# A hand-planned decoder trunk on one core: whole PSUM banks as dependences, top-k steps moved between two attentions, and a planned margin on results that TensorE takes

## The chip, the cores and the metric

The kernel runs on one core of a Trainium2 chip. The metric is the device time of one execution in microseconds (us). Engines: TensorE (PE; PEld is its weight load), VectorE (DVE), ScalarE (ACT), GpSimd (POOL) and SyncE (SP), which here issues DMAs. TensorE writes its results to PSUM, which has eight banks of 512 floats per partition; VectorE and ScalarE read them there.

## The reference

A decoder trunk of two layers over 512 positions with a residual stream of 1024 channels, in float32. Each layer does, on the normalised stream:

```python
z = rmsnorm(x, norm_g[i]) @ w_in[i]          # one projection, split into all inputs below
o_a = diff_attention(...)     # A: 4 heads, each softmax map 0 - lam * softmax map 1, RMSNorm per head
o_b = dsa_attention(...)      # B: an indexer scores the keys, top 128 of them per query, 8 heads
o_c = nsa_attention(...)      # C: compressed blocks + selected blocks + window, 8 heads, sigmoid gates
up = einsum('bsnw,nwd->bsnd', stack([o_a*silu(a_g), o_b*silu(b_g), o_c*silu(c_g)], 2), w_up[i])
x = x + sum(sigmoid(merge) * up, axis=2) @ w_out[i]
x = x + (p[i] @ w_ple[i]) * sigmoid(rmsnorm(x, ple_norm_g[i]) @ w_ple_gate[i])
```

The top 128 keys of B are found by 16 rounds that take the eight largest scores of each query and strike them out.

## The kernel before

The stream lies transposed, channels on partitions, in eight tiles of 128 x 512. Every float32 operand of a large matmul is split into a high and a low part (`whi`, `wlo` for weights, `HI`, `LO` for the stream, `PTh`, `PTl` for probabilities), and a product is three matmuls. The high part of a weight is a copy by ScalarE or GpSimd, the low part a subtraction by GpSimd or VectorE.

The order of work is written by a planner, `Plan`. The kernel's text records operations in a sequence (`add`), with a cost for each and the operations it must come after; that is found from boxes (`box`: partitions from and to, columns from and to) of the cells that each operation reads or writes in a tile (`meet`). Writers and readers whose boxes meet are ordered. All TensorE operations on one tile are ordered anyway (`filler`). Then `put_down` (line 387) makes the time table: at each step it takes the operation that can start earliest on any engine; for engines other than TensorE a rank (its place in the sequence) is added with a small weight, TensorE takes of the ready ones that with the lowest rank. `o.ready` is the planned time at which an operation may start, set by the ends of those it depends on; a tile's slot in a ring of buffers is released apart from that. An operation listed for two engines (`VG`: GpSimd or VectorE, `AG`: ScalarE or GpSimd) goes to the one that would end it first. The table's order of each engine is what the chip runs; semaphores for the true dependences are added when the operations are put down.

The sequence of a layer: projections for the indexer and the token values; `index_scores`; `attend_a` for four heads (A); `attend_c` for four tiles of queries with two groups and two maps each (C); `attend_b` for four pairs of heads (B); then output projections. Each attention is woven (`weave`) with projections that do not depend on it (`proj`, `merge`, `rise`), in `mm` banks (3), while the attention's scores, transposes and sums take `at` banks (5).

Places that the prediction speaks of. `weigh_a`, inside `attend_a` (from line 1085), transposes a head's probabilities and sums the values into one bank `po`, four blocks of 128 columns by 1, 2, 3 and 4 matmuls (two records each in the trace); ScalarE reads each block into `o`, squares it, GpSimd makes the inverse root (`rsqrt`), ScalarE scales `o`, and later `turn` transposes it:

```python
T.matmul(po[:, i * P : (i + 1) * P], at[:, j * P : (j + 1) * P],
         AV[j][:, h * P : (h + 1) * P], start=j == 0, stop=j == i)
...
A.activation(on[:, i * P : (i + 1) * P], po[:, i * P : (i + 1) * P], AF.Copy,
             scale=rr[:, 0, i : i + 1])
```

`topk` (line 1059) is a generator of 51 steps a layer: 48 of a maximum and a replacement on VectorE (16 rounds over three blocks of queries), and three that turn the marks into masks for B. `background(n)` (line 1072) takes n of them, with the rank set back by 400; `attend_a` calls it with `A_TOPK[i]` for each query block i of a map, `softmax` with `C_TOPK[i]` in C. What is left is taken before `attend_b`. `c_query` writes an unrotated query `t` by VectorE and multiplies it with the compressed keys (`at<-KCb,t`).

Of the kernel before, what the change touches and what calls it, by code (L numbers as in the profile page):

```python
# [25 lines left out]
ROUNDS = 16  # L26
NQB = 6
PV_LAG = 3
A_TOPK = (0, 0, 1, 1)
C_TOPK = (0, 0, 1, 1)  # L30
NRAW = 4
NWS = 4
NKB = 10
URGE = 0.002
WARM = 9
THETA = 500000.0

# [89 lines left out]
class View:  # L127
# [23 lines left out]

    def box(self):

        a, b = int(self.cells[(0,) * self.cells.ndim]), int(self.cells[(-1,) * self.cells.ndim])
        w = self.tile.width
        return a // w, b // w, a % w, b % w
# [7 lines left out]
    def put_down(self):  # L164
        x = self.tile.put_down()
        for kind, a, b in self.steps:
            if kind == "getitem":
                x = x[a]
            elif kind == "rearrange":
                x = x.rearrange(a, **b)  # L170
            elif kind == "bitcast":
                x = x.bitcast(a)
            else:
                x = x.to_broadcast(a)
        return x
# [43 lines left out]
class Plan:  # L219
# [52 lines left out]
    def add(self, names, call, args, kw):  # L272
# [15 lines left out]
        for x in op.ins:  # L288
            box = x.box()
            for b, w in x.tile.writes:  # L290
                if self.meet(b, box):
                    op.after.add(w)
        for x in op.outs:
            box, t = x.box(), x.tile
            for line in (t.writes, t.reads):
                for b, w in line:
                    if self.meet(b, box):
                        op.after.add(w)
# [88 lines left out]
    def put_down(self):  # L387
        names = ("tensor", "vector", "scalar", "gpsimd", "sync")
        free = dict.fromkeys(names, 0.0)
        port = wire = 0.0  # L390
        held = {(e, o.seq): self.shares(e, o) for o in self.ops for e in o.engines}

        def begin(e, op):
            at = max(free[e], op.ready)
            return max(at, port - 0.14) if held[e, op.seq] else at

        can = {e: [] for e in names}
        slots = {r: [(0.0, k) for k in range(self.size[r])] for r in self.rings}
        line = {r: list(t) for r, t in self.rings.items()}

        def enter(op):
            if op.left == 0:
                for e in op.engines:
                    can[e].append(op)

        def give(ring):
            while line[ring] and slots[ring]:
                t = line[ring].pop(0)
                at, t.slot = min(slots[ring])
                slots[ring].remove((at, t.slot))  # L410
                for op in t.users:
                    op.ready = max(op.ready, at)
                    op.left -= 1
                    enter(op)

        def finish(e, op):

            at = begin(e, op) + self.cost(e, op)[0]
            return at + sum(o.us for o in can[e] if o.rank < op.rank and len(o.engines) == 1 and o.ready <= at)

        for r in line:
            give(r)
        done = 0
        while done < len(self.ops):
            best = None
            for e in names:
                pick = None
                for op in can[e]:
                    at = begin(e, op)
                    key = at + (0.0 if e == "tensor" else URGE) * op.rank  # L430
                    if pick is not None and (pick[2], pick[1].rank) < (key, op.rank):
                        continue
                    if len(op.engines) > 1 and e != min(op.engines, key=lambda x: finish(x, op)):
                        continue
                    pick = (at, op, key)
                if pick and (best is None or pick[0] < best[0]):
                    best = (pick[0], e, pick[1])
            if best is None:
                raise RuntimeError("the plan is stuck")
            at, e, op = best  # L440
            us, lag = (op.us, op.lag) if e == op.engines[0] else self.cost(e, op)
            op.engine, op.start = e, at
            free[e] = at + us
            if held[e, op.seq]:
                port = at + us
            for x in op.engines:
                can[x].remove(op)
            done += 1
            end = at + us + lag
            if op.call == "dma_start":  # L450
                tile = (op.outs + op.ins)[0]
                end = wire = max(end, wire) + 0.1 + tile.shape[0] * tile.columns() * 4 / 370000.0
            for o in op.next:
                o.ready = max(o.ready, at + us if o.engines == (e,) and op.call != "dma_start" else end)
                o.left -= 1
                enter(o)
            for t in op.tiles.values():
                t.uses -= 1
                t.end = max(t.end, end)
                if t.uses == 0 and t.space != "dram":  # L460
                    slots[t.ring].append((t.end, t.slot))
                    give(t.ring)
        E = mybir.EngineType
        with self.tc.manual_schedule(engines={E.PE, E.DVE, E.Activation, E.Pool, E.SP}):
            for op in sorted(self.ops, key=lambda o: (o.start, o.seq)):
                real = [a.put_down() if isinstance(a, View) else a for a in op.args]
                kw = {k: a.put_down() if isinstance(a, View) else a for k, a in op.kw.items()}
                call = op.call
                if call == "copy" and op.engine == "gpsimd":
                    call, real = "tensor_scalar", real + [1.0, 0.0, ALU.mult, ALU.add]  # L470
                getattr(getattr(self.nc, op.engine), call)(*real, **kw)  # L471
# [3 lines left out]
def trunk_kernel(ctx, tc, xT, xN, pT, pos, freq, W, WK, small, con, out):  # L475
# [38 lines left out]
    def at_ps():  # L514
        return ps("at", 5)
# [18 lines left out]
    spare = at_ps()  # L534
    for _ in range(WARM):
        T.matmul(spare[:, :P], ones, ones, start=True, stop=True)
# [125 lines left out]
    for l in range(L):  # L662
# [178 lines left out]
        def causal(i):  # L841
            return mask[:, 384 - i * P : 512]

        def softmax_parts(pt, i, sc, m, st):

            n = P * (i + 1)
            blk = pt[:, POFF[i] : POFF[i] + n]
            mn = sb("mx", (P, 1), bufs=8)
            V.tensor_tensor_reduce(blk, sc[:, :n], m, 1.0, -NEG, ALU.add, ALU.min, mn)
            A.activation(blk, blk, AF.Exp, bias=mn, scale=-1.0, accum_out=st[:, i : i + 1])  # L850
# [221 lines left out]
        def background(n):  # L1072

            plan.shift = 400
            for _ in range(n):
                next(chain, None)
            plan.shift = 0
# [7 lines left out]
        def attend_a(h):  # L1085
            pts, sts = [], []
            for c in range(2):
                pt = sb("P", (P, 1280), bufs=3)
                st = sb("st", (P, NQ), bufs=4)
                for i in range(NQ):  # L1090
                    sc = sc_ps()
                    qk(sc, have["AQ", h][c], have["AK", h, c], i)
                    softmax_parts(pt, i, sc, causal(i), st)
                    background(A_TOPK[i])
                    yield QK_US[i]
# [64 lines left out]
        def softmax(q, k, masks, factor):  # L1160
# [3 lines left out]
            for i in range(NQ):  # L1164
# [3 lines left out]
                if masks is masks_c:  # L1168
                    background(C_TOPK[i])
                yield QK_US[i]  # L1170
# [359 lines left out]
```

## Time and profile before

| | before |
|---|---|
| time, median of 3 runs | 1411.82 us (1410.4 to 1412.04) |
| the profiled execution | 1409.82 us |
| its span, first to last instruction | 1408.0 us |
| TensorE busy, instructions | 1378.9 us (98%), 6882 matmul records |
| VectorE busy | 1046.4 us (74%) |
| ScalarE busy | 790.3 us (56%) |
| GpSimd busy | 567.3 us (40%) |

All rows come from the one profiled execution. Nearly every operation is recorded by one helper line, so groups are told apart by tile names ("out<-in"). A matmul's recorded length is longer than its distance to the next, since matmuls are pipelined; a stall shows as a larger distance between starts, and in part as idle time.

### The profile page before, as it was taken

Reading aid. Unit: us, or ns where it says so; the run is one execution under the profiler, and the core shown is the slowest. Engines: PE = TensorE matmul, PEld = TensorE weight load, DVE = VectorE, ACT = ScalarE, POOL = GpSimd, SP = SyncE. Lnnn points to the kernel's source line nnn. Section 1 sums busy time; section 2 is a strip of 40 time slices with the busy share of each in tenths; the row PEclk is TensorE's granted clock in tenths of the full one; section 3 lists DMA queues with packets and bytes.
Section 4 is the critical chain, followed back from the end, with each engine's and each line's share of the span. In section 5 each row is a group of like instructions: output and inputs, shape, how many; then the busy total and the mean of one; then the engine's idle time right before and its main releaser. Section 6 shows DMA issues by size and latency. Waiting matters only on the chain.

```text
span 1408.0 us, 20777 instructions
## 1 busy us (share of the span) xinstructions
PE 1378.9 (98%) x6882; PEld 1153.3 (82%) x6882; DVE 1046.4 (74%) x2348; ACT 790.3 (56%) x1831; POOL 567.3 (40%) x613
## 2 busy tenths in 40 slices
PE   9999999999999999999999999999999999999997
PEld 7888877888888888888887888778888888888886
DVE  7688888888887566555785888897888855666566
ACT  6455655866764356334444656567677734643443
POOL 3464466545343152122251744774445322313040
PEclk9999999999999999999999999999999999999998
DMA  6223221111222221342422231312112222124221
GB/s 246 98 83 101 72 89 62 61 61 53 75 68 83 85 88 61 106 149 98 147 83 97 83 98 52 106 55 67 60 61 68 76 83 89 62 75 157 97 91 68
DMA packets 67932, 123.65 MB, mean 88 GB/s; under 512 B 7920, under 2 KB 10224, under 8 KB 67824
## 3 DMA queue, kind: packets, MB, share of 16 engines
q1 hardware_dynamic: 62640, 113.14, 24.5%
q10 hardware_dynamic: 5184, 9.18, 1.9%
q8 instruction: 54, 0.88, 0.2%
q14 instruction: 54, 0.44, 0.1%
HBM read 117.57 MB, written 4.72 MB: 87 GB/s over the span
## 4 chain that ended last, share of the span: by engine, by line
PE 89%; DVE 5%; ACT 1%; issue 1%; POOL 0%; DMA 0%; DVEq 0%; POOLq 0%; ACTq 0%; SPq 0%
PE mm L471 70%; PE at L471 19%; DVE t L471 1%; DVE nt L471 0%; DVE P L471 0%; POOL nt L471 0%; DVE cm L471 0%; DMA raw<-W 0%; DVE K L471 0%; DVE rstd L471 0%; ACT o L471 0%; DVE g L471 0%; DVE wlo L471 0%; DVE x L471 0%; DVE hr L471 0%
## 5 line engine op out<-in xcount | busy, mean ns | idle before, releaser
L471 PE MATMUL mm<-HI,whi 128*128 128x512 f32 x1240 | 496.9, 401 | 2.1 <-POOL whi L471 1.1
L471 PE MATMUL mm<-HI,wlo 128*128 128x512 f32 x1240 | 488.7, 394 | 1.6 <-DVE wlo L471 1.0
L471 PE MATMUL mm<-LO,whi 128*128 128x512 f32 x1240 | 488.0, 394 | 1.3 <-DVE LO L471 1.3
L471 POOL TENSOR_SCALAR whi<-raw 128x512 fp32r<-128x512 f32 (+1 forms) x191 | 130.5, 684 | 535.2 <-PE mm L471 357.2
L471 POOL TENSOR_TENSOR wlo<-raw,whi 128x512 fp32r<-128x512 f32 (+1 forms) x191 | 256.9, 1348 | 188.0 <-ACT whi L471 151.6
L471 PEld LDWEIGHTS mm<-HI,wlo 128*128 128x128 f32 x1240 | 233.9, 189 | 51.0 <-DVE wlo L471 1.4
L471 PEld LDWEIGHTS mm<-HI,whi 128*128 128x128 f32 x1240 | 234.3, 189 | 41.8 <-POOL whi L471 1.6
L471 ACT CAST whi<-raw 128x512 fp32r<-128x512 f32 (+1 forms) x205 | 125.2, 614 | 254.8 <-PE mm L471 185.5
L471 PEld LDWEIGHTS mm<-LO,whi 128*128 128x128 f32 x1240 | 234.4, 189 | 40.0 <-DVE LO L471 2.3
L471 DVE TENSOR_TENSOR wlo<-raw,whi 128x512 fp32r<-128x512 f32 (+1 forms) x205 | 149.7, 735 | 79.6 <-ACT whi L471 43.9
L471 ACT ACTIVATE P<-P,mx 128x512 f32<-128x512 f32 (+3 forms) x256 | 142.4, 557 | 65.7 <-DVE mx L471 64.6
L471 PE MATMUL at<-K,Q 128*128 128x256 f32 (+3 forms) x608 | 138.9, 325 | 0.0
L471 PEld LDWEIGHTS at<-K,Q 128*128 128x128 f32 x608 | 103.1, 189 | 16.1 <-issue 0.5
L471 DVE TENSOR_TENSOR t<-mm,R 128x512 f32<-128x512 f32 (+1 forms) x101 | 69.0, 683 | 61.1 <-PE mm L471 57.8
L471 DVE CUSTOM_DVE_ANT_0 P<-at,consts 128x128 f32<-128x128 f32 x208 | 93.8, 470 | 21.6 <-PE at L471 20.5
L471 DVE TENSOR_TENSOR PTl<-at,PTh 128x512 fp32r<-128x512 f32 x192 | 87.0, 484 | 28.2 <-ACT PTh L471 21.6
L471 POOL TENSOR_TENSOR Q<-t,Q 64x512 fp32r<-64x512 f32 x64 | 87.5, 1367 | 34.9 <-ACT Q L471 29.3
L471 PE MATMUL at<-consts,P 128*128 128x128 f32 x560 | 96.1, 272 | 0.8 <-ACT PTh L471 0.7
L471 ACT ACTIVATE P<-P,rc 128x128 f32<-128x128 f32 x192 | 92.0, 552 | 7.9 <-DVE rc L471 6.9
L471 ACT CAST PTh<-at 128x512 fp32r<-128x512 f32 x192 | 74.4, 420 | 38.4 <-PE at L471 31.1
L471 PEld LDWEIGHTS at<-consts,P 128*128 128x128 f32 x560 | 71.5, 140 | 22.1 <-ACT PTh L471 1.3
L471 PE MATMUL mm<-BRh,whi 128*128 128x512 f32 x192 | 77.0, 405 | 0.5 <-DVE t L471 0.5
(222 smaller groups left out, 2126.5 us busy)
## 6 DMA issues: line engine op xcount, KB each, us to landing
raw<-W SPq DMA_DIRECT2D x396, 256.0 KB, 2.6
raw<-WK SPq DMA_DIRECT2D x16, 176.0 KB, 2.3
X<-xT ACTq DMA_DIRECT2D x10, 256.0 KB, 4.1
res<-X ACTq DMA_DIRECT2D x8, 256.0 KB, 2.0
X<-res ACTq DMA_DIRECT2D x8, 256.0 KB, 3.4
out<-K SPq DMA_DIRECT2D x8, 256.0 KB, 2.5
X<-xT SPq DMA_DIRECT2D x6, 256.0 KB, 4.8
P<-xN SPq DMA_DIRECT2D x3, 512.0 KB, 6.0
```

The costliest lines, as they stand in the source:

```text
L471: getattr(getattr(self.nc, op.engine), call)(*real, **kw)
```

## The change

Three edits. A PSUM tile's box is now the whole tile, so a read of some of its columns depends on earlier writes of others. The selection takes no step in A, and three steps a map instead of two in C. In the time table an operation of TensorE that depends on one of VectorE, ScalarE or GpSimd is ready 0.6 us after the planned end of that one.

```diff
-A_TOPK = (0, 0, 1, 1)
-C_TOPK = (0, 0, 1, 1)
+A_TOPK = (0, 0, 0, 0)
+C_TOPK = (0, 1, 1, 1)
...
+SLACK = 0.6
...
     def box(self):
 
+        if self.tile.space == "psum":
+            return 0, self.tile.shape[0] - 1, 0, self.tile.width - 1
         a, b = int(self.cells[(0,) * self.cells.ndim]), int(self.cells[(-1,) * self.cells.ndim])
...
             for o in op.next:
-                o.ready = max(o.ready, at + us if o.engines == (e,) and op.call != "dma_start" else end)
+                late = SLACK if o.engines[0] == "tensor" and e in ("vector", "scalar", "gpsimd") and op.call != "dma_start" else 0.0
+                o.ready = max(o.ready, at + us if o.engines == (e,) and op.call != "dma_start" else end + late)
```

## Rows read from the trace of the kernel before

**Rows 1.** The page's first part: busy us, share of the span, instructions.
```profile
PE 1378.9 (98%) x6882; PEld 1153.3 (82%) x6882; DVE 1046.4 (74%) x2348; ACT 790.3 (56%) x1831; POOL 567.3 (40%) x613
```
**Rows 2.** Busy time by stage: stretch, length, engines (instructions), granted clock, DMA share, GB/s.
```profile
112.00:244.00 132.00, 125.62 (x657) 104.38 (x656) 112.51 (x272) 77.95 (x205) 74.96 (x98) 0.99 0.25 80
244.00:431.00 187.00, 186.50 (x995) 156.95 (x995) 157.25 (x437) 129.65 (x339) 84.05 (x94) 1.00 0.19 63
431.00:560.00 129.00, 129.00 (x637) 107.47 (x636) 82.64 (x173) 70.01 (x162) 41.65 (x41) 1.00 0.24 80
...
803.00:936.00 133.00, 128.48 (x683) 107.52 (x682) 115.24 (x278) 82.65 (x215) 76.71 (x101) 1.00 0.26 84
936.00:1122.00 186.00, 185.53 (x986) 155.81 (x985) 156.58 (x440) 130.87 (x341) 84.35 (x91) 1.00 0.19 63
```
**Rows 3.** Waits of TensorE, us, times, longest: 112 to 244, then whole span.
```profile
PE at L471 <- ACT o L471: 2.0, 4, 0.6
PE at L471 <- DVE t L471: 1.6, 1, 1.6
PE mm L471 <- DVE wlo L471: 1.0, 1, 1.0
PE mm L471 <- POOL whi L471: 0.9, 1, 0.9
PE mm L471 <- DVE hr L471: 0.4, 1, 0.4
PE at L471 <- ACT PTh L471: 0.4, 1, 0.4
...
PE at L471 <- ACT o L471: 4.0, 8, 0.6
PEld at L471 <- ACT o L471: 8.3, 15, 1.1
```
**Rows 4.** Timeline (start, length, idle before), TensorE and `o`; last, all transposes of `o`.
```profile
148.52 0.38 PE L471 MATMUL at<-X,PTh 128*128 128x128 f32 x2
148.94 0.37 ACT L471 ACTIVATE o<-at,rr 128x128 f32<-128x128 f32 x1 [0.28 <-PE at L471]
149.36 0.49 PE L471 MATMUL at<-X,PTh 128*128 128x128 f32 x2 [0.46 <-ACT o L471]
...
182.49 1.05 PE L471 MATMUL at<-X,PTh 128*128 128x128 f32 x8
...
L471 PE MATMUL at<-consts,o x12: 270/272/330, 162.4 to 242.9; 128*128 128x128 f32 x12
```
**Rows 5.** Timeline around the longest wait in A.
```profile
227.87 2.52 POOL L471 TENSOR_TENSOR wlo<-raw,whi 128x512 fp32r<-128x512 f32 x2
228.11 1.09 DVE L471 TENSOR_TENSOR cm<-cm,gate 128x8 f32<-128x8 f32 x1
229.12 0.68 DVE L471 MAX8 m<-acc 128x8 f32<-128x512 f32 x1
230.34 0.68 DVE L471 TENSOR_TENSOR t<-mm,R 128x512 f32<-128x512 f32 x1
231.07 0.66 PE L471 MATMUL at<-KCb,t 128*128 128x64 f32 x4 [1.59 <-DVE t L471]
```
**Rows 6.** Busy time by stretch, as rows 2, after that wait.
```profile
228.00:240.00 12.00, 10.41 (x50) 8.34 (x48) 11.40 (x26) 4.95 (x11) 9.47 (x17) 0.86 0.13 45
```
**Rows 7.** The selection's instructions on `acc`: ns min/median/max, first and last start.
```profile
L471 DVE MAX8 m<-acc x96: 413/550/691, 111.9 to 1117.7; 128x8 f32<-128x256 f32 x32, 128x8 f32<-128x384 f32 x32, 128x8 f32<-128x512 f32 x32
L471 DVE MATCH_VALUE_LOAD acc<-m,acc x96: 60/86/93, 112.4 to 1118.4; 128x8 f32 x96
L471 DVE MATCH_REPLACE8 acc<-m,acc x96: 401/543/689, 112.4 to 1118.5; 128x256 f32<-128x256 f32 x32, 128x384 f32<-128x384 f32 x32, 128x512 f32<-128x512 f32 x32
```
**Rows 8.** `wlo` on VectorE from 244 to 431; a stretch of full VectorE, as rows 2.
```profile
L471 DVE TENSOR_TENSOR wlo<-raw,whi x11: 681/692/695, 281.6 to 429.8; 128x512 fp32r<-128x512 f32 x11
...
196.00:208.00 12.00, 12.00 (x57) 9.84 (x55) 11.45 (x22) 5.67 (x12) 11.34 (x10) 1.00 0.37 116
```

## Prediction

> **What bounds the kernel now.** I read the busy times first, then the busy time by stage, then what TensorE waits for, then the timeline around two of these waits. TensorE has a matmul running for 98% of the span, VectorE 74%, ScalarE 56%, GpSimd 40% [rows 1]. So the time is TensorE's own stream plus the places where it stands still, and a change that leaves every matmul as it is can win or lose such places alone. The stages tell where they lie [rows 2]: the differential attention (A) of the first layer, 112 to 244 us, has 132 − 125.62 = 6.4 us without a matmul, that of the second, 803 to 936 us, 133 − 128.48 = 4.5 us; the compressed attention (C), 244 to 431 and 936 to 1122 us, has 0.5 us each, and the sparse attention (B) behind it none. The busy share of an engine over the whole span hides this: VectorE works 85% of A (112.51 of 132) and 84% of C (157.25 of 187), nearly alike, yet only A loses time.
>
> What A waits for stands in [rows 3]: in the first layer ScalarE's `o` (4 times, 2.0 us), VectorE's `t` (one of 1.6), `wlo` 1.0, `whi` 0.9, `hr` 0.4, `PTh` 0.4, together 6.3 of the 6.4 us. The second layer has 4.5 us by its stage row; `o` has 4.0 us in 8 waits over the whole span.
>
> **Part 1, bank boxes.** In `weigh_a` four groups of matmuls fill four column blocks of one PSUM tile `po`, and ScalarE reads each block into `o`. [rows 4] show what happens when a read is placed between two groups: matmuls into `po` at 148.52, ScalarE's read of a block at 148.94 for 0.37 us, the next matmuls into the same bank at 149.36, with 0.46 us idle put down to that read, though they write other columns. Without a read between them 8 such matmul records take 1.05 us in a row, and two take 0.38, so (1.05 − 0.38) / 6 = 0.11 us from one to the next, 0.22 for two, and 0.27 for the length of one [rows 4]: the start came 0.84 after the last pair, a loss of 0.62, of which 0.46 shows as idle and 0.16 lies under the tail of the matmul before. How many: of the 8 waits for `o`, two are of another kind, the 0.62 us before the transposes of `o` in each layer; 4.0 − 2 × 0.62 = 2.8, which is six of 0.46. The weight loads wait for `o` 15 times [rows 3], 7 times more than the matmuls; these are covered in part by a running matmul, and I bound them by 0 and 0.27 each (one matmul's length), and take 0.15. With whole banks as boxes the planner puts all reads behind the last group, so the waits go: 6 × 0.62 + 7 × 0.15 = **4.7 us**, bounds 3.7 and 5.6.
>
> What it adds is a later start of four reads of `o`: ScalarE reads block 0 after all 20 matmul records, 20 × 0.11 = 2.2 us later. Behind them on ScalarE wait its squares of `o` and then GpSimd's inverse root; the transposes of `o` take that result. In the trace the first read starts at 148.94, the first of these transposes at 162.4 [rows 4], with projections between: hidden, and if that cover is gone it costs at most the 2.2 us once a head, 17.6 in all; I take nothing, since the planner also knows the later time. Other PSUM tiles are read only after their last matmul already, so there this part is without effect.
>
> **Part 2, the selection.** One step of `topk` issues three VectorE instructions, a maximum, a value load and a replacement: means by the medians of [rows 7] 0.550 + 0.086 + 0.543 = 1.18 us, no DMA and nothing on another queue. 16 steps a layer (4 heads, 2 maps, 2 steps) leave A, 16 go to C (4 tiles, 4 maps, one more): 16 × 1.18 = 18.9 us; the total of 48 and the three that remain for the end stay. VectorE in A falls from 112.5 to 93.6 of 132 us (71%), in C it rises from 157.3 to 176.1 of 187 (94%), less what the planner moves: 11 of C's `wlo` subtractions are on VectorE, and GpSimd, 45% busy there, may take them: 11 × 0.692 = 7.6 us [rows 2, 8], which leaves 90%.
>
> What that is worth in A is read from its longest wait [rows 5]. The unrotated query `t` is written by VectorE at 230.34, and TensorE's `at<-KCb,t` starts at 231.07 after 1.59 us idle. Ahead of `t` on VectorE are a maximum of 0.68 us at 229.12, and the replacement and value load of another step (0.543 + 0.086), 1.3 us in all: without the steps most of this wait is gone. After it the granted clock was 0.86 over 228 to 240 us [rows 6], that is part of the stretch at the lower of its two levels (1.2 GHz): 12 × 0.14 = 1.7 us. The second layer's A has it at 1.00 throughout [rows 2], so this term is there once.
>
> The same rows show a small operation `cm<-cm,gate` on 8 columns take 1.09 us while GpSimd runs two `wlo` of 2.52 us in all [rows 5]. The Trainium skill, "SBUF — State Buffer", § Who interferes with whom, says that a VectorE instruction with two SBUF inputs contends with a GpSimd instruction that reads SBUF, and that the second one blocks until the first has finished; the rounds have one input, so by that rule they add only their own length, but `wlo` moved to GpSimd in C would give back part of the 7.6 us that they free. With half of a 1.29 us `wlo` lost eleven times, 7.1 us, VectorE in C would stand at 94% instead of 90%; the row agrees with the rule, and this speaks against the change (it belongs to the slower rival).
>
> **Part 3, the margin.** It changes no instruction and adds no wait on the chip; in the planner's book a TensorE operation that takes a result of VectorE, ScalarE or GpSimd counts as ready 0.6 us later, so other ready matmuls are put ahead of it. It does not act on the release of a bank. Costs: where TensorE has nothing else to do the order stays the same, so nothing there; where it has, the delayed operation comes up to 0.6 us later, which C and B hide as long as projections are at hand (they have next to no idle time now [rows 2]). The other places where TensorE waits (start, change of layer, end) have no other work, and I leave them as they are, with ±1.5 us for the new order.
>
> **Parts 2 and 3 together in A.** Waits other than the six of part 1: idle 6.4 + 4.5 − 2.8 = 8.1 us; ten waits (six in the first layer, four in the second) each with 0.16 us hidden, 1.6; the clock, 1.7; together 11.4 us. The ones of up to about 0.6 (`o`, `hr`, `PTh`, in both layers): 2 × (0.62 + 0.4 + 0.4) + 6 × 0.16 = 3.8 us, inside the margin, gone. `t`: 2 × (1.6 + 0.16) + 1.7 = 5.2 us, gone by 1.3 us of steps and 0.6 of margin. `wlo` and `whi`, 1.0 and 0.9, lose 0.6 each: 1.2. Sum 10.2. A list made anew puts some other operation just late, so I take four fifths of it: **8.2 us**, bounds 0 (the lateness moves on) and 11.4.
>
> **C after the move.** At 84% VectorE C loses 0.5 us a layer, A at 85% loses 3.0 us to VectorE's `t`, `wlo` and `hr`. A stretch at 95% VectorE without TensorE idle exists (11.45 of 12 us, TensorE 12.00) [rows 8], so 90 to 94% does not decide by itself. I take less than half of A's 3.0, 1.3 a layer, **2.6 us** lost, because the margin works there too; bounds −1.0 (the present 0.5 twice is gone) and +22.6 (below).
>
> **The sum.** −4.7 − 8.2 + 2.6 = −10.3 us. The profiled execution took 1409.82 us, of which 1408.0 are span; that is 2.0 below the median of the three runs, 1411.82, and below all of them. Its successor would be at 1399.5, a median at **1401.5**.
>
> **Rivals.**
> - *VectorE becomes the bound of C (slower).* For: 94% if nothing moves. VectorE's 29.75 us idle in C are waits for TensorE and ScalarE in a fixed order; if the rounds can't fill them, its chain grows by 18.9 us a layer, less the 7.6 of `wlo`: 11.3, twice 22.6; with the gains 4.7 + 8.2 that is +9.7: 1421.5. It decides from where VectorE, late by more than the 0.6 us margin, holds banks that TensorE needs; at half the price it is −1.6, near no change. Against: 95% without idle in [rows 8], steps that nothing waits for before B, and B with VectorE at 64% (82.64 of 129) into which they can run over.
> - *Part 1 alone counts.* The lateness in A is of the order as a whole and reappears elsewhere: −4.7 and ±2, 1407.
> - *No change.* The bank waits go but the new order loses as much at other places, or C gives back what A wins: 1409 to 1414.6.
> - *All of it.* Every wait of A gone, and C free: 5.6 + 11.4 + 1.0 = 18, 1393.8.
>
> **How the numbers follow.** Chances: the forecast (1397 to 1406) 0.50, part 1 alone (1405 to 1409) 0.17, no change 0.13, slower 0.12, all of it 0.08. About 0.2% (2.8 us) is what a measurement of this kernel can tell from no change. Faster by more, below 1409.0: 0.50 + 0.17 + 0.08 = 0.75; same 0.13; slower 0.12. The range from 1394 to 1413 leaves out the slower case, the top of no change and the last of the gains, less than 2 in 10.
>
> **What would show it.** Part 1: no wait of TensorE for `o` before `at<-X,PTh`, and the reads of `o` of a head in one row after its last matmul. Part 2: no maximum before about 244 us, VectorE at 70 to 75% in A, 90 to 94% in C, and there at most some 2 us of TensorE idle a layer. Parts 2 and 3: `at<-KCb,t` without a wait over 0.3 us, no granted clock below 1.00 in A. I am wrong if C shows many waits for `P`, `PTl` or `t` of VectorE (the first rival), or if A still has some 4 us idle a layer, only at other tiles (part 1 alone).

## The result, and the profile after

The changed kernel takes 1394.82 us in the median of 4 runs (1394.02 to 1395.80), the kernel before 1411.11 in the median of its 4 (1410.0 to 1412.04): ratio 0.9885, 95% interval 0.9868 to 0.9902, 16.3 us faster. The profiled executions took 1409.82 and 1395.80 us, with spans of 1408.0 and 1394.0, so the two traces show 14.0 of the 16.3 us. One kernel's executions differ with their mean granted clock: in 34 timings of the kernel before, those at 0.994 took 1412.3 to 1415.1 us, those at 0.998 1408.7 to 1410.9.

Busy time by stage of the changed kernel; the columns are those of [rows 2], and the first two rows begin ahead of A. The second layer runs some 10 us earlier than before, so the last two stretches end a little further into the next stage.

```profile
0.00:12.00 12.00, 9.32 (x34) 7.33 (x35) 5.77 (x10) 7.69 (x13) 2.25 (x9) 0.86 0.85 289
0.00:112.00 112.00, 106.37 (x498) 89.17 (x499) 84.21 (x165) 62.48 (x122) 52.61 (x53) 0.98 0.42 140
112.00:244.00 132.00, 130.18 (x698) 109.69 (x697) 114.38 (x289) 84.32 (x228) 78.02 (x112) 1.00 0.26 82
244.00:431.00 187.00, 187.00 (x989) 157.37 (x988) 155.59 (x418) 124.77 (x318) 82.25 (x82) 1.00 0.21 67
...
803.00:936.00 133.00, 131.42 (x709) 110.81 (x708) 115.33 (x288) 87.56 (x237) 79.53 (x113) 1.00 0.26 82
936.00:1122.00 186.00, 186.00 (x979) 156.75 (x978) 155.54 (x421) 119.89 (x305) 78.47 (x79) 1.00 0.20 67
```

Beside [rows 2]: A stands still for 1.8 and 1.6 us instead of 6.4 and 4.5, C not at all instead of 0.5 and 0.5. That is 8.5 us; over the whole span idle time falls by 7.9 (29.1 to 21.2). The granted clock is 1.00 through A, where it had fallen once [rows 6]; but it falls by as much in the first 12 us, 0.86, where the kernel before had 1.00. The mean granted clock is 0.996 in both profiled executions, so it explains next to none of the 14.0 us. TensorE's busy time fell by 6.1 us (1378.9 to 1372.8) with the same 6882 matmul records. That I put down to the part of a wait that [rows 4] show as covered, under the tail of the matmul before it, where it counts as busy; it was not measured wait by wait.

What TensorE waits for in the first layer's A, as [rows 3]:

```profile
PE mm L475 <- POOL whi L475: 0.7, 1, 0.7
PE at L475 <- DVE o L475: 0.6, 1, 0.6
PE mm L475 <- DVE t L475: 0.3, 1, 0.3
PE at L475 <- DVE mx L475: 0.2, 1, 0.2
```

No wait names ScalarE's `o` any more; VectorE's `o` in this list is the read of the transposed sums, whose bank the next scores wait for. Where the reads of `po` are now is seen from the first head's last matmuls (timeline) and the reads of A (tile view: ns min/median/max, first and last start):

```profile
153.87 1.05 PE L475 MATMUL at<-X,PTh 128*128 128x128 f32 x8
...
L475 ACT ACTIVATE o<-at,rr x16: 345/348/370, 155.3 to 236.9; 128x128 f32<-128x128 f32 x16
```

The first read begins at 155.3 us, not at 148.94 as in [rows 4], behind the head's last matmul. The long wait of [rows 5] before `at<-KCb,t` is gone too. But the selection did not do what its two tuples say. Its instructions on `m` in A and in C, before and then after (columns: stretch, length, busy us (instructions), clock, DMA share, GB/s; three instructions a step):

```profile
112.00:244.00 132.00, 18.12 (x49) 0.99 0.25 80
244.00:431.00 187.00, 35.57 (x94) 1.00 0.19 63
```

```profile
112.00:244.00 132.00, 12.19 (x33) 1.00 0.26 82
244.00:431.00 187.00, 40.31 (x106) 1.00 0.21 67
```

16 steps lay in A before and 11 lie there now, so 5 were moved, not 16.

### The profile page after: what moved, and what is told of

Its sections match the earlier page's. It is cut to its first block, busy times and chain, and to the rows that moved or that the text cites. A ratio compares the mean times of both kernels' runs of the same rounds, so it can differ in the third digit from the quotient of the medians.

```text
span 1394.0 us, 20799 instructions
## 1 busy us (share of the span) xinstructions
PE 1372.8 (98%) x6882; PEld 1151.7 (83%) x6882; DVE 1050.0 (75%) x2357; ACT 788.2 (57%) x1828; POOL 556.7 (40%) x607
## 5 line engine op out<-in xcount | busy, mean ns | idle before, releaser
L475 POOL TENSOR_SCALAR whi<-raw 128x512 fp32r<-128x512 f32 (+1 forms) x194 | 134.2, 692 | 525.7 <-PE mm L475 411.5
L475 POOL TENSOR_TENSOR wlo<-raw,whi 128x512 fp32r<-128x512 f32 (+1 forms) x186 | 249.7, 1346 | 198.8 <-ACT whi L475 168.8
L475 DVE TENSOR_TENSOR PTl<-at,PTh 128x512 fp32r<-128x512 f32 x192 | 86.7, 483 | 35.3 <-ACT PTh L475 24.6
```

## The experiments

Each run was timed beside the kernel before on the same chip; ratios are to those runs, with their 95% interval. "Idle in A" is the length less TensorE's busy time in 112 to 244 and 803 to 936 us.

| run | median, us | before beside it | ratio (interval) | idle in A, us |
|---|---|---|---|---|
| before | 1411.11 | | | 6.4 + 4.5 |
| all three parts | 1394.82 | 1411.11 | 0.9885 (0.9868 to 0.9902) | 1.8 + 1.6 |
| boxes alone | 1397.24 | 1410.52 | 0.9907 (0.9893 to 0.9922) | 2.3 + 1.5 |
| tuples alone | 1405.51 | 1410.52 | 0.9968 (0.9953 to 0.9982) | 5.1 + 3.4 |
| margin alone | 1398.25 | 1410.52 | 0.9914 (0.9900 to 0.9929) | 1.7 + 1.7 |
| boxes and margin | 1397.17 | 1410.52 | 0.9905 (0.9891 to 0.9920) | 2.6 + 2.7 |
| boxes and tuples | 1398.63 | 1412.08 | 0.9907 (0.9890 to 0.9925) | 2.3 + 2.5 |
| rank weight 0.0019 | 1408.07 | 1412.08 | 0.9972 (0.9960 to 0.9985) | 5.6 + 4.1 |
| rank weight 0.0021 | 1410.11 | 1412.08 | 0.9984 (0.9971 to 0.9997) | 7.0 + 5.5 |
| all, steps held in C | 1393.55 | 1412.08 | 0.9871 (0.9854 to 0.9887) | 1.5 + 1.8 |
| boxes for heads 0, 1 | 1399.73 | 1410.29 | 0.9920 (0.9900 to 0.9940) | 3.9 + 1.8 |
| boxes for heads 2, 3 | 1402.88 | 1410.29 | 0.9947 (0.9926 to 0.9967) | 3.9 + 3.3 |
| all, margin 1.2 | 1397.28 | 1410.29 | 0.9903 (0.9886 to 0.9920) | 1.1 + 0.9 |
| held, margin 1.2 | 1398.60 | 1410.29 | 0.9914 (0.9897 to 0.9930) | 1.3 + 1.3 |

**One part alone.** The theory was the prediction's: each part takes its own waits, so the parts add. The rival: one of them does all of it, and what is credited to the others is the same time counted twice.

```diff
# box_alone
     def box(self):
+        if self.tile.space == "psum":
+            return 0, self.tile.shape[0] - 1, 0, self.tile.width - 1
```

> The kernel before with the whole-bank boxes alone; no step of the selection is moved and there is no margin. By the prediction's part 1 the waits of TensorE for `o` before `at<-X,PTh` go and the time falls by 4.7 us (3.7 to 5.6), to about 1406.4, with the other waits of A still there (`t` 1.6 us in each layer). The rival, that the lateness only moves on, gives within 2 us of before, 1409 to 1413, with the idle time of A about 6.4 and 4.5 us as before at other tiles.

Measured: 13.3 us faster, nearly three times the term. TensorE's stages in A, and the waits of both layers that name `o`:

```profile
112.00:244.00 132.00, 129.73 (x703) 109.17 (x701) 116.39 (x301) 87.80 (x237) 75.68 (x108) 1.00 0.26 80
803.00:936.00 133.00, 131.54 (x713) 110.41 (x712) 118.00 (x300) 89.08 (x238) 76.72 (x110) 1.00 0.27 81
...
PE at L473 <- ACT o L473: 1.4, 3, 0.6
```

Idle time in A falls by 7.2 us, of which 2.6 are waits for `o`; the rest are `t`, `wlo` and `hr` of [rows 3], which have nothing to do with `po`. VectorE works more in A than before (116.4 against 112.5 us), so it is not a lighter VectorE that ended them. TensorE's weight loads wait for `o` 6 times, 3.7 us, instead of 15 times, 8.3 us [rows 3].

```diff
# topk_alone
-A_TOPK = (0, 0, 1, 1)
-C_TOPK = (0, 0, 1, 1)
+A_TOPK = (0, 0, 0, 0)
+C_TOPK = (0, 1, 1, 1)
```

> The kernel before with the two tuples of the selection changed alone. By the prediction 16 steps a layer leave A, the wait for `t` falls from 1.6 us to about 0.3 and the second wait for the clock goes: 3 to 6 us faster, 1405 to 1408, less up to 3 us in C. The rival: the planner draws steps back into A wherever VectorE has nothing else ready, as the trace after shows 11 and 10 of them there; then A loses 5 or 6 steps only, and this alone is within 3 us of before, 1408 to 1414.

Measured: 5.0 us faster, by its numbers the first theory's 3 to 6, but the runs with another rank weight below put a value on a mere new table that lies close to it. The wait for `t` is gone, the waits for `o` are not (10, 5.0 us). VectorE ahead of `t`, beside [rows 5]:

```profile
228.21 1.06 DVE L471 TENSOR_TENSOR cm<-cm,gate 128x8 f32<-128x8 f32 x1
229.30 0.17 DVE L471 TENSOR_TENSOR cm<-cm,consts 128x8 f32<-128x8 f32 x1
229.44 0.69 DVE L471 TENSOR_TENSOR t<-mm,R 128x512 f32<-128x512 f32 x1
```

`cm<-cm,gate` is as long as before, the operation behind it took 0.69 us there, and no maximum or replacement lies here from 219 to 230 us. For this one wait the move did what the prediction said.

```diff
# slack_alone
+SLACK = 0.6
...
-                o.ready = max(o.ready, at + us if o.engines == (e,) and op.call != "dma_start" else end)
+                late = SLACK if o.engines[0] == "tensor" and e in ("vector", "scalar", "gpsimd") and op.call != "dma_start" else 0.0
+                o.ready = max(o.ready, at + us if o.engines == (e,) and op.call != "dma_start" else end + late)
```

> The kernel before with the margin of 0.6 us alone. By the prediction the waits of A up to 0.6 us go (3.8 us), those over it lose 0.6 each (about 4 us in all), and the waits for a bank between the blocks of `po` stay, since the box does not know of them: 1403 to 1406. The rival, that the margin does all that part 1 and the moved steps are credited with, gives about 1397 or less.

Measured: 12.3 us faster, near the rival. The waits for `o` were to stay; of TensorE's list over the whole span

```profile
PE at L473 <- ACT o L473: 1.4, 5, 0.5
PE at L473 <- DVE PTl L473: 1.3, 4, 0.6
```

shows 1.4 us in 5 waits where there were 4.0 in 8 [rows 3]. A later planned start of the matmuls into `po` also takes some of them out from between the reads, without knowing of the bank: of the six waits for a read of `po` two are left at their full 0.46 us (at 181.97 and 867.21 us) and two at 0.19 and 0.18 (209.89 and 895.43). So parts 1 and 3 act in part on the same waits.

`box_slack` has both edits, and the tuples as before.

> Boxes and margin, without the move of the selection. If the moved steps are worth nothing (the planner puts them where VectorE is free anyway) this equals the changed kernel, 1393 to 1397. By the prediction, where the steps ahead of `t` make most of its wait, 3 us and more are missing: 1398 to 1401.

Measured: 13.4 us, no more than the boxes alone (1397.17 and 1397.24, timed side by side). All three parts give 0.9885 against 0.9905; the intervals overlap, so the third's worth on top is some 0.2% at most and not told from nothing. `box_topk` has the boxes and the tuples, without the margin.

> Boxes and moved selection without the margin. Boxes alone took 13.3 us, the margin added to them 0.1. If the margin acts on waits that the boxes' table has lost already, this equals the changed kernel, 1393 to 1396.5. If the margin is needed where the steps come into C, some waits of VectorE appear there and it is 1397 or more.

Measured: 0.9907, 2 us over the upper end of what I wrote for a margin without effect, though C has at most 0.4 us idle a layer; by the ratio it equals the boxes alone, and it has one stretch at the lower clock in the first layer's A. The terms do not add: 13.3, 5.0 and 12.3 alone, 16.3 together.

**A table laid anew.** Any edit to the planner moves hundreds of instructions. What does that alone do?

```diff
# urge_0019, and urge_0021 with 0.0021
-URGE = 0.002
+URGE = 0.0019
```

> The kernel before with the planner's weight of the rank 0.0019 instead of 0.0020, none of the three parts. It stands for nothing but a table that is laid anew. If the parts remove lateness by what they do, this stays within 3 us of before, 1408 to 1414, with waits for `o` before `at<-X,PTh` in 5 to 8 places and another few waits of VectorE in A. If the table of before was merely an unlucky one, whose wait for `t` any other table loses, it is 5 us faster or more, 1406 or less, though the waits for `o` stay.

> As the run with 0.0019, with 0.0021: the other side. Within 3 us of before by the first theory, 1406 or less by the second; the two together give the size of what a new table alone does.

Measured: 4.0 and 2.0 us faster. The waits of A with 0.0019, and then with 0.0021 (first layer):

```profile
PE at L471 <- ACT o L471: 2.0, 4, 0.6
PE mm L471 <- POOL whi L471: 1.2, 1, 1.2
PE mm L471 <- DVE wlo L471: 1.0, 1, 1.0
PE at L471 <- DVE t L471: 1.0, 1, 1.0
```

```profile
PE at L471 <- DVE t L471: 1.7, 1, 1.7
PE at L471 <- ACT o L471: 1.6, 3, 0.6
PE mm L471 <- POOL whi L471: 1.1, 1, 1.1
PE mm L471 <- DVE wlo L471: 1.0, 1, 1.0
```

The list is nearly that of [rows 3], with `t` at 1.0 or 1.7: by this wait the table of before was not just an unlucky one. 2 to 4 us is the step by which these tables differ anyway, as far as two tables tell. The tuples alone, at 5.0, are not told from it (0.9968 and 0.9972).

**Are the rounds harmless in C?** In the changed kernel most steps never left A. Here they must:

```diff
# steps_held: the changed kernel, in topk()
+            gate_op = None
...
-                    V.max(m8, a)
+                    if gate_op is None:
+                        gate_op = next(o for o in reversed(plan.ops) if o.engines[0] == "tensor")
+                    op = V.max(m8, a)
+                    if gate_op not in op.after:
+                        op.after.add(gate_op)
+                        gate_op.next.append(op)
+                        op.left += 1
```

> The changed kernel with one more dependence: no step of the selection may start before the scores of the first map of C, so that all 48 are truly in C (in the changed kernel 11 and 10 still lie in A). By the prediction's term for C VectorE is at 90 to 94% there and C loses 1.3 us a layer, while A gains at most 1: 1395 to 1398. The slower rival, VectorE bounding C, gives up to 11 us a layer, with `P`, `PTl` or `t` named in C's waits: 1400 to 1417.

Measured: 1393.55 us, 0.9871. The selection in A and C, and the stages:

```profile
112.00:244.00 132.00, 0.00 (x0) 1.00 0.27 82
244.00:431.00 187.00, 52.34 (x138) 1.00 0.21 67
```

```profile
112.00:244.00 132.00, 130.46 (x702) 110.34 (x700) 103.39 (x258) 85.62 (x233) 77.39 (x111) 1.00 0.27 82
244.00:431.00 187.00, 187.00 (x991) 157.43 (x990) 164.31 (x445) 124.53 (x316) 90.56 (x87) 1.00 0.21 67
```

No step is in A, 46 are in C up to 431 us, VectorE works 88% of C (164.31 of 187), and TensorE has no idle time there. The slower rival is gone with this, and the loss of 1.3 us a layer that I had for C did not come either: the time is below the 1395 to 1398 of that term. A gains next to nothing by it either: 1.5 and 1.8 us idle against 1.8 and 1.6. This is the fastest version run, but its interval and the changed kernel's overlap.

**Where do the boxes get 13 us from?** Writing "the reads of `po` depend on its last matmul" into `weigh_a`, without a change to `box`, gives the same instructions in the same order on each engine as the boxes alone; the boxes do nothing else in this kernel. So the dependence can be put on two heads at a time.

```diff
# heads_0_1 (heads_2_3: h >= 2)
+                last = po.tile.filler
                 for i in range(NQ):
-                    A.activation(on[:, i * P : (i + 1) * P], po[:, i * P : (i + 1) * P], AF.Copy,
-                                 scale=rr[:, 0, i : i + 1])
+                    op = A.activation(on[:, i * P : (i + 1) * P], po[:, i * P : (i + 1) * P], AF.Copy,
+                                      scale=rr[:, 0, i : i + 1])
+                    if h < 2 and last not in op.after:
+                        op.after.add(last)
+                        last.next.append(op)
+                        op.left += 1
```

> The kernel before; in `weigh_a` the reads of `po` depend on its last matmul for heads 0 and 1 alone (for all four heads this gives the very order of instructions of the boxes alone, which took 13.3 us where the prediction had 4.7). If each wait for `o` is worth only itself, two of 0.62 a layer go, 2.5 us, and with a new table's 2 to 4 us the time is 1404 to 1409. If an early gap between TensorE and its table is what makes later results late, the waits for `t` and `hr` of head 3's stretch go too: 1398 to 1402.

> The same for heads 2 and 3 alone. Each wait worth itself: 0.21 + 0.27 + 0.62 + 0.27 a layer, 2.7 us, and a new table's 2 to 4: 1404 to 1409. If the reads put late by these two heads are what moves `t` and `hr` (they lie in the same stretch, 208 to 244 us), these waits go here and not with heads 0 and 1: 1400 to 1403, with the waits for `o` of heads 0 and 1 (0.62 each) and for `wlo`, `whi` still there.

Measured: 10.6 and 7.4 us faster. The waits of the first layer's A with heads 0 and 1, and then with heads 2 and 3:

```profile
PE mm L471 <- POOL whi L471: 1.8, 1, 1.8
PE at L471 <- ACT o L471: 1.1, 2, 0.7
PE mm L471 <- ACT whi L471: 0.5, 1, 0.5
```

```profile
PE at L471 <- ACT o L471: 1.6, 3, 0.6
PE mm L471 <- DVE wlo L471: 1.0, 1, 1.0
PE mm L471 <- POOL whi L471: 0.9, 1, 0.9
```

`t` and `hr` are off this list in both, also where the only repaired waits lie in other heads; with heads 2 and 3 `t` comes back in the second layer with 0.8 us. `wlo` goes with heads 0 and 1 only, and `whi` grows there from 0.9 to 1.8. The two halves sum to 18.0 us, more than the 13.3 of both, but only just by the intervals, and their profiled spans, 8.5 and 5.8 us shorter, sum to 14.3. So neither of the two theories holds as I wrote it: with heads 0 and 1 the gain is more than the waits themselves and a new table's 2 to 4 us, with heads 2 and 3 (7.4 where these give up to 6.7) that is not clear, and in neither does the surplus stay in the stretch of its head.

**The table and the trace.** A kernel's text fixes its planner's table, so the planned starts can be set beside the trace, engine by engine in their order. Shown are the planned end of the last matmul, how far TensorE runs behind the table near there (median of the matmuls planned for 1362 to 1368 us) and the span of the profiled execution:

| run | planned end, us | behind it, us | span, us |
|---|---|---|---|
| before | 1372.4 | 26.8 | 1408.0 |
| all three parts | 1370.1 | 14.6 | 1394.0 |
| boxes alone | 1367.2 | 18.9 | 1394.8 |
| tuples alone | 1370.2 | 24.6 | 1403.4 |
| margin alone | 1376.3 | 10.8 | 1395.9 |
| boxes and margin | 1374.3 | 10.9 | 1394.4 |
| boxes and tuples | 1367.2 | 21.9 | 1397.8 |
| rank weight 0.0019 | 1374.0 | 24.5 | 1407.1 |
| rank weight 0.0021 | 1370.7 | 29.8 | 1409.1 |
| all, steps held in C | 1370.1 | 12.9 | 1391.9 |
| boxes for heads 0, 1 | 1369.1 | 21.7 | 1399.5 |
| boxes for heads 2, 3 | 1370.5 | 23.1 | 1402.2 |
| all, margin 1.2 | 1376.6 | 8.8 | 1394.3 |
| held, margin 1.2 | 1376.6 | 12.2 | 1397.7 |

Of the boxes' 13.2 us by span, 5.2 are a table that is shorter as planned, and 7.9 are less lateness; why that table is shorter is not shown. Lateness grows in A: over the first layer's A by 10.5 us before, by 3.6 with the boxes. The margin alone makes the table 3.9 us longer and takes 16.0 us of lateness away.

**A larger margin.** `margin_1200` is the changed kernel with `SLACK = 1.2`, `steps_held_1200` the one with held steps and 1.2.

> The changed kernel with a margin of 1.2 us instead of 0.6. If what is left in A (0.5 to 0.9 us at six places a layer) is lateness against the table, it goes, 2 to 4 us: 1390 to 1393. If these places have no other ready matmul, nothing changes: 1393 to 1396. If the margin begins to hold buffers too long, C or B show idle time: over 1396.

> The kernel with all 48 steps held back to C, and a margin of 1.2 us. Held steps alone gave 0.9871 of before, about 1.5 us less than the changed kernel. With lateness left in A this goes to 1389 to 1392; without, it stays at 1392 to 1395; with buffers held too long, over 1395.

Measured: 0.9903 and 0.9914, 2.5 and 5 us over their counterparts with 0.6 by the medians. The first of these is not told from nothing (the intervals of 0.9903 and 0.9885 overlap, and the spans are 1394.3 and 1394.0); the second is, by intervals that do not meet (0.9914 and 0.9871). Idle time in A falls to 1.1 and 0.9 us, but at the change of layer it grows. The stretch from 664 to 803 us with 0.6 and, in the second fence, with 1.2, where its longest wait is shown too:

```profile
664.00:803.00 139.00, 136.23 (x644) 115.28 (x643) 107.70 (x177) 67.79 (x130) 58.48 (x51) 1.00 0.31 102
```

```profile
664.00:803.00 139.00, 134.50 (x635) 113.67 (x634) 106.26 (x170) 67.08 (x127) 62.67 (x55) 1.00 0.32 102
...
PE at L475 <- ACT t L475: 1.7, 1, 1.7
```

4.5 us idle against 2.8, with a wait of 1.7 us for `t` that the smaller margin has not. What is left in A is lateness that a margin can take away, as the first theory had it, and the longer margin costs as much elsewhere, in neither of the stages that I had named: beside the changed kernel its table is 6.5 us longer, and the lateness 5.8 less.

## Why the prediction was right or wrong

- **What bounds the kernel**: right. The matmuls are the same, and what moved are the places where TensorE stands still, nearly all in A.
- **Sign and size**: faster, as forecast; 16.3 us where the sum had 10.3, inside the range but at its lower end (1394.8 beside 1394.0). The case that came is the one called "all of it", with a chance of 0.08: A nearly free and C free.
- **Part 1, the mechanism**: right. The reads stand behind the last matmul, the waits before `at<-X,PTh` are gone, and the later start of `o` costs next to nothing: with the boxes alone the transposes of `o` wait for it 1.4 us in all, before 1.2. **Its size** was wrong: 4.7 us forecast, 13.3 alone. All six waits were of 0.62 us from start to start, as priced; the step that failed is that the sum stopped there and took the rest of the table to stay as it was. The new table is 5.2 us shorter, and waits for `t`, `wlo` and `hr` went with it.
- **Part 2, "16 steps leave A"**: wrong. 5 left in the first layer. I read the tuples as places; they are only places in the sequence, and the planner starts a later operation on an engine that has nothing nearer to do, as VectorE has at times in A. VectorE's work in A went up to 114.4 us, not down to 93.6. What I said of the wait for `t` fared better. In the tables without a margin each wait for `t` in A over 0.5 us (before, 0.0019 and 0.0021 in both layers, heads 2 and 3 in the second) has a maximum or a replacement within 4 us ahead of `t`, and also a small `cm` operation of 0.79 to 1.18 us that takes 0.17 elsewhere. The tuples alone took away the first and kept the second, and the wait went. I had counted only the steps, and had taken only the tuples to move them: the boxes alone, with A_TOPK as before, happen to have neither there.
- **Part 3 and the sum**: the margin alone takes 12.3 us and adds 0.1 to the boxes. I gave the waits for `o` to part 1 and the others to parts 2 and 3 and added the terms. The runs show that parts 1 and 3 each reach most of both lists. That the time lies in the range owes something to luck: part 1 was too small by 8.6 us, and parts 2 and 3 add some 3 to it, by intervals that overlap, not 8.2.
- **The term for C**: 2.6 us lost was forecast, nothing was lost. With all steps truly there VectorE is at 88% and TensorE has no idle time. The stretch at 95% in [rows 8] was the better guide than A's 3.0 us. Nor did `wlo` go to GpSimd as I supposed: VectorE does 13 of them in the first layer's C, before 11, and 7 with the steps held.
- **The clock**: the drop behind `t` is gone, as said, but the changed kernel's trace has one as long at its start, so the term of 1.7 us is not in the gain that the traces show. Nor does a drop hang on `t` alone: with weight 0.0019, and with boxes and tuples, the first layer's A drops right behind a wait for `whi` (1.2 and 0.8 us); with 0.0021 both layers drop, 0.86 over the 12 us around `t`.
- **What would show it**: no wait for `o` before `at<-X,PTh`, no long wait for `at<-KCb,t` and no clock below 1.00 in A came true; "no maximum before 244 us", "70 to 75% VectorE in A" (87%) and "90 to 94% in C" (83%) did not.

**Open**: why a repair at two heads also ends the wait for `t` at another. In part the new table does it: in the first layer with heads 0 and 1, as with the boxes alone, neither a step nor a long `cm` stands ahead of `t`. With heads 2 and 3 both stand there, and the wait is 0.1 us in the first layer and 0.8 in the second. That two tables with another weight kept the wait does not say how often a new table would lose it; why the boxes' table is shorter, and why `hr` and `wlo` went, was not followed. That the chip falls behind its table in A is so, by 10.5 us over the first. But at the end of it all four engines are behind by nearly the same, 11.6 to 11.9 us, and with the tuples alone the wait for `t` went though the waits for `o` had grown. So lateness by itself does not make the next wait.

## What to carry to other kernels

Where an order is planned by hand, a dependence that the program's semaphores keep and the plan does not know can be worth more than the waits that it shows: six waits of 0.62 us and some smaller ones, repaired, gave 13 us, of which 5 were a table that was shorter as planned, for reasons not shown. Do not add the terms of edits that work on the same plan; run each alone and together, and run a neutral change of the plan beside them, to know what a new order alone is worth (here 2 to 4 us, by two tries). Where the planner's own times are at hand, set them beside the trace: they part a shorter plan from a plan that is better kept. And a place in the sequence is not a place in time: look in the trace where a moved step really went.

## What the runs showed of the hardware

A matmul into a bank waited for ScalarE's read of other columns of that bank, at a cost of 0.62 us each of the six times. It waits for a semaphore that the read sets; what the bank would do without one, no run shows.

Three small VectorE operations ahead of the first layer's wait for `t` took 1.28, 1.09 and 0.69 us instead of some 0.17, and each ended within 0.04 us of the end of a GpSimd subtraction. The first of them, before TensorE's wait for `hr` (timeline):

```profile
218.51 1.29 POOL L471 TENSOR_TENSOR wlo<-raw,whi 128x512 fp32r<-128x512 f32 x1
218.55 1.28 DVE L471 COPY hr<-x 128x31 f32<-128x31 f32 x1
```

The clock fell to the lower of its two levels behind single short waits: after 1.6 us for `t` in the first layer before (0.86 over 12 us), after 0.8 us for `whi` with boxes and tuples, where the next matmuls of 512 columns start 0.43 us apart instead of 0.23. The same wait of 1.6 us in the second layer left it at 1.00, so the length of one wait does not decide. Two such matmuls of the kernel with boxes and tuples (timeline: start, length, idle before):

```profile
135.13 0.63 PE L473 MATMUL mm<-HI,whi 128*128 128x512 f32 x1 [0.82 <-POOL whi L473]
135.56 0.63 PE L473 MATMUL mm<-LO,whi 128*128 128x512 f32 x1
```

VectorE at 88% of a 187 us stage, in a fixed order, cost TensorE nothing.
